# A decoder step on one core: the attention's results pass through DRAM, the modulation is spread over more products, one operand split is moved

## The chip, the cores and the metric

The program runs on one core of a Trainium2 chip. The metric is the device time of one execution in microseconds. A core has five engines with a queue of instructions each: PE (TensorE, matrix products), ACT (ScalarE), DVE (VectorE), POOL (GpSimd) and SP (SyncE, which here only issues transfers). ACT and POOL can issue transfers too. Results of PE land in PSUM, in banks; all other data on the chip lies in SBUF.

## The reference

One layer of a hybrid decoder, for 512 prompt tokens and 64 decoded tokens (8 sequences of 8), model width 1024:

- A modulation vector is made from the conditioning: `mod = silu(c) @ w_ada + b_ada`, cut into six parts of 1024 (shift, scale and gate of the first half of the layer, and of the second).
- `h = rmsnorm(x) * (1 + sc1) + sh1`, then one projection `h @ w_in`, cut into three operands of a gated convolution, queries, keys, values, and two gate logits.
- The convolution branch: `u = c_gate * xa`, a causal convolution of width 3 over tokens, times `b_gate`, then `@ w_conv_out` gives `ya`.
- The attention branch: 16 heads on 4 key heads, window 128, one learned sink for each head, distance bias; the result `o` (1024 wide) goes through `@ w_attn_out` to `yb`.
- `mixed = sigmoid(ga) * ya + sigmoid(gb) * yb`, and `x = x + g1 * (mixed @ w_mix_out)`.
- A second modulated norm, an up-projection to 2 x 2816, a convolution on one half, GELU, product with the other half, the down-projection, the gated residual, and a last norm.

All in float32. The decoded tokens also attend to a cache of 128 rows for each sequence.

## The kernel before

**Products.** PE has no full float32 product in one pass here. Each operand is split into a high part (rounded to PE's type) and a low part (what is left), and a product is three passes: high x high, high x low, low x high. `split` does it: one copy on ACT makes the high part, one subtraction on DVE the low part. Activations are kept transposed (features on the 128 partitions, the 576 tokens in the free dimension), so that 1024 features are 8 tiles of 128 x 576.

Most products are made in pairs by `pair_product` (a Winograd-like scheme: seven partial products of half size in place of eight). One pair makes two output tiles of 128 x 576 in seven parts, each of 4 x 3 matmuls of 288 columns into one of three banks X, Y and Z; after each part something is taken out of a bank (`minus`, `out_a0`, `out_b1` ...). The parts use sums and differences of weight halves (`pair_weights`, `prepare`) and of operand halves (`PairOperands`, `EarlyOperands`, `RawOperands`). The order is X a0, Z s1, Y s2, X a1, Y s3, Z s4, Y b1. A dictionary of steps says what ACT, DVE and POOL are given before the first part (key 0) and after each part (keys 1 to 7).

**The list of pairs.** `jobs` has 27 pairs (I number them from 0). Pairs 0 to 7 are gates and queries, 8 to 19 make the inner values and gates of the convolution, 20 to 22 the last gates, and 23 to 26 are `w_conv_out`. After them come eight plain products (`product`) with `w_attn_out`, which read the eight operands `o`, then the mix, the second norm and the feed-forward part. Pair n loads the weights of pair n + 2 and prepares those of pair n + 1.

**The filler.** Attention and modulation are written as generators. `pair_product` calls `tick(2)` once in each part, 14 ticks for a pair; `product` calls `tick` once for each of its 8 k. Each tick adds a rate to a counter, and for each whole number the generator runs one step. In the pairs the generator is `beside_conv`: the attention first (rates 0.28 and 0.45), then `modulation(2048)` at rate 0.6. The modulation reads 2048 columns of `w_ada` in 32 loads of 128 x 512 (256 KB), one for each step, and after every eight loads, five steps behind the last of them (`ROWS_AHEAD`), PE multiplies them (`side_by_side`, line 1264). The whole takes 44 steps. The second call, `modulation(4096)`, begins in pair 26, at rate 0.6.

**The buffers.** Nearly all temporary tiles come from one pool of 54 buffers of 128 x 576 float32 (`slot`, `A_BUFS`). A planner orders the instructions and hands out the buffers at build time: a buffer goes to the next tile in the order of the program, and the instruction that writes it first waits until all readers of the tile before are done. The queue of an engine is executed in order, so whatever stands behind such an instruction waits too. PE is held in the order of the program from the first pair on, ACT and DVE from pair 14 on (`N_ATT`). Weights have a pool of their own with 4 raw buffers (`W_BUFS`); an SP load of weights waits for one of them.

**The attention's results.** `prompt_values` (line 1160) writes the results of one key head for 4 blocks of 128 tokens into two tiles `ot`, eight in all, by ACT copies of 128 x 128 (line 1179). They are made in pairs 2 to 11. The decoded tokens' results go to a tile `od`. Both wait until pair 26, where `part_o` (line 1542) copies the 64 columns of `od` into each `ot` on POOL and splits it into `o` by ACT and DVE. So eight of the 54 buffers hold `ot` from the attention to pair 26.

**The early operands.** Before pair 0 a plain product makes the second query tile. Behind it stand four calls `op.n3()` (line 1495): each splits one quarter operand of `h` (128 x 288), which only the fifth part (Y s3) of the pairs reads.

Of the kernel before, what the change touches and what calls it, by code (L numbers as in the profile page):

```python
# [10 lines left out]
F32 = mybir.dt.float32  # L11
# [5 lines left out]
P = 128  # L17
D = 1024
NK = D // P
SEQ = 512  # L20
# [54 lines left out]
def step_kernel(ctx: ExitStack, tc: tile.TileContext, ins: dict, outs: list):  # L75
    nc = tc.nc
# [7 lines left out]
    dp = ctx.enter_context(tc.tile_pool(name="dp", bufs=1, space=bass.MemoryType.DRAM))  # L84
# [6 lines left out]
    def nm(s):  # L91
        cnt[0] += 1
        return f"{s}{cnt[0]}"

    def slot(s, dt=F32, shape=None):
        return ap_.tile(shape or [P, NT], dt, tag="a", name=nm(s))
# [7 lines left out]
    def aux():  # L104
        return pa.tile([P, 512], F32, tag="aux", name=nm("aux"))
# [25 lines left out]
    def pv(t):  # L131
        return t[:, 0:512]

    def sv(t):
        return t[:, 512:576]
# [7 lines left out]
    def split(hi, lo, src):  # L143

        act.activation(hi, src, AF.Copy)
        dve.tensor_tensor(out=lo, in0=src, in1=hi.bitcast(F32), op=ALU.subtract)

    def split_slot(src, s):
        hi, lo = slot(s + "h", F32R), slot(s + "l", F32R)
        split(hi, lo, src)  # L150
        return hi, lo
# [7 lines left out]
    def split_w(raw):  # L159
        nk = raw.shape[1]  # L160
        hi = wp.tile([P, nk, P], F32R, tag="whi", name=nm("whi"), bufs=S_BUFS)
        lo = wp.tile([P, nk, P], F32R, tag="wlo", name=nm("wlo"), bufs=S_BUFS)
        split(hi, lo, raw)
        return (lambda k: hi[:, k, :]), (lambda k: lo[:, k, :])
# [24 lines left out]
    filler = []  # L189
# [685 lines left out]
    def vt(i):  # L875
        return V[i // 2][:, i % 2, :]
# [6 lines left out]
    made, early_ops = {}, []  # L883
# [42 lines left out]
    def queries(t, q):  # L926

        hd, g2 = t // 2, t % 2
        for par in range(2):
            mine = HALF[par]  # L930
            dst = qS[:, hd // 2, :, :, par, g2, :] if par == hd % 2 else qX[:, hd // 2, :, :, g2, :]
            nc.vector.tensor_copy(
                out=dst[mine], in_=sv(q)[mine].rearrange("p (q b t) -> p q b t", q=2, b=4)
            )
        QS[t] = q
        ready[hd] = ticks[0] + Q_TICKS
        if g2 == 1:
            par = 1 - hd % 2
            for q in range(2):
                nc.gpsimd.dma_start(  # L940
                    qS[HALF[1 - par], hd // 2, q, :, par, :, :].rearrange("p b g t -> p b (g t)"),
                    qX[HALF[par], hd // 2, q].rearrange("p b g t -> p b (g t)"),
                )
# [20 lines left out]
        out=sel,  # L964
        in0=snk.rearrange("p (h g) -> p h g", h=4),
        in1=ind.unsqueeze(1).to_broadcast([P, 4, 4]),
        op=ALU.mult,
# [22 lines left out]


    pinned.append(pe)
    ot = []
    od = []

    def softmax_steps(s, n, sinks, nsinks, w):

# [161 lines left out]

    def prompt_values(parts):  # L1160
        O = aux()
        while len(ot) < 2 * parts[-1][0] + 2:
            ot.append(slot("ot"))
        for u, (hd, i, pts) in enumerate(parts):
            nkt, c = len(pts), slice(256 * u, 256 * u + 256)
            for n in range(2 * nkt):
                kt, par = n // 2, n % 2
                done = nc.tensor.matmul(  # L1168
                    O[HALF[par], c],
                    vt(i - nkt + 1 + kt)[:, hd * 64 : hd * 64 + 64],  # L1170
                    pts[kt][:, par * 256 : par * 256 + 256],
                    start=(kt == 0), stop=(kt == nkt - 1),
                )
                if u + n:
                    tc.keep_in_program_order(done)
        for u, (hd, i, pts) in enumerate(parts):
            for g in range(2):
                at = 256 * u + P * g
                nc.scalar.copy(ot[2 * hd + g][:, i * P : i * P + P], O[:, at : at + P])

    def attention():
        units = [(hd, i) for hd in range(4) for i in range(4)]
        s, pts = {}, {}
        for n in range(len(units) + 3):
            if n == CACHE_AT:
                cache_load(0)
            if n < len(units):
                hd, i = units[n]
                while 2 * hd + 1 not in QS or ticks[0] < ready[hd]:
                    yield False  # L1190
                s[n] = prompt_scores(hd, i)
            if n >= 4 and n % 2 == 0:
                prompt_values([(*units[u], pts.pop(u)) for u in (n - 4, n - 3)])
            yield False
            if 2 <= n <= len(units) + 1:
                pts[n - 2] = prompt_turn(units[n - 2][1], s.pop(n - 2))
            yield False
        filler[1] = .45
        before = None
        for n in range(3):  # L1200
            s, more = [], []
            if n < 2:
                yield from decode_scores(n, s, more)
            if before is not None:
                yield from before
            before = decode_values(n, s, more)
# [64 lines left out]
    def modulation(c0):  # L1271

        ps = aux()
        cols = [[None] * 4 for _ in range(NK)]
        for n in range(4 * NK + ROWS_AHEAD):
            if n < 4 * NK:
                k, j = n // 4, n % 4
                cols[k][j] = slot("ada", shape=[P, 512])
                c = c0 + 512 * j
                nc.sync.dma_start(cols[k][j], ins["w_ada"][0, k * P : k * P + P, c : c + 512])  # L1280
            yield False
            done = n + 1 - ROWS_AHEAD
            if done > 0 and done % 8 == 0:
                side_by_side(ps, (done // 4 - 2, done // 4 - 1), cols)
                yield False
        row = slot("row", shape=[P, 512])
        nc.scalar.copy(row, ps)
        yield False
        t = aux()
        yield False  # L1290
        for cc in range(4):
            transpose(t[:, cc * P : cc * P + P], row[:, cc * P : cc * P + P], ident)
        b0 = c0 // P
        nc.vector.tensor_tensor(
            out=modT[:, b0 : b0 + 16, :].rearrange("p (j c) r -> p j c r", j=4),
            in0=t.rearrange("p (c j r) -> p j c r", c=4, j=4)[:, :, :, 0:9],
            in1=parT[:, b0 : b0 + 16]
            .rearrange("p (j c) -> p j c", j=4)
            .unsqueeze(3)
            .to_broadcast([P, 4, 4, 9]),  # L1300
            op=ALU.add,
        )
        yield False
# [4 lines left out]

    def beside_conv():
        yield from attention()  # L1310
        filler[1] = .6
        yield from modulation(2048)
        yield True

# [79 lines left out]
    ya, w_next, raw_ao, o, late = [], {}, {}, [], []  # L1394
# [41 lines left out]
    def branch(m0, m1):  # L1436
        return Job(w_in, m0 * P, made, lambda: branch_outs(m0, m1), (m1 - m0) * P)

    def inner_job(m):
        return Job(w_in, 1024 + m * P, made, lambda: inner_outs(m), 1024)  # L1440

    def gate_job(n):
        x, c, m = (1, 5632, 2 * n) if n < 4 else (0, 4608, 2 * n - 8)
        return Job(w_in, c + m * P, made, lambda: gate_outs(x, m))

    def query_job(at):
        qt = [slot("q") for _ in range(2)]

        def outs():
            a0, a1, b0, b1 = copy_outs(qt, HD**-0.5)  # L1450

            def last(ps):
                b0(ps)
                for n in range(2):
                    queries(2 * at + n, qt[n])

            return a0, a1, last, b1

        return Job(w_in, Q0 + 2 * at * P, made, outs, scale=HD**-0.5)

    jobs = [
        gate_job(0), query_job(1), gate_job(1), gate_job(2), query_job(2), gate_job(3), gate_job(4),
        query_job(3), inner_job(0), inner_job(4), branch(0, 4), inner_job(1), inner_job(5), branch(1, 5),
        inner_job(2), inner_job(6), branch(2, 6), inner_job(3), inner_job(7), branch(3, 7),
        gate_job(5), gate_job(6), gate_job(7),
    ]
# [25 lines left out]
    q1 = slot("q")  # L1492
    nc.scalar.activation(q1, ps, AF.Copy, scale=HD**-0.5)
    queries(1, q1)
    for op in early_ops:
        op.n3()
    stT = state_in(st_conv, "stT", NK)
    a = aux()
    transpose(a[:, :74], par2, ident[:74, :74])
# [31 lines left out]
    for n in range(4):  # L1531
# [2 lines left out]
                1: [lambda n=n: late[2 * n - 2]()], 2: [lambda n=n: late[2 * n - 1]()],  # L1534
            }
    jobs[-1].after = {
        2: [lambda: part_o(2)], 3: [lambda: part_o(3)],
        4: [lambda: w_next.update({1: split_w(w_raw)})], 5: [lambda: part_o(4)], 6: [lambda: part_o(6)],
        7: [lambda: part_o(8)],
    }  # L1540

    def part_o(n):
        for k in range(len(o), n):
            nc.gpsimd.tensor_copy(out=sv(ot[k]), in_=od[0][:, k, :])
            o.append(split_slot(ot[k], "o"))

    for n, job in enumerate(jobs):
        if n == N_ATT:
# [490 lines left out]
    for m0, m1 in FCH:  # L2039
# [31 lines left out]
        if m1 < NF:  # L2071
# [3 lines left out]
            n = m1 - m0  # L2075
# [47 lines left out]
    jobs = [Job(w_dn[FB * P :, :], m * P, made3, lambda m=m: mix_outs(m, 40)) for m in range(0, NK - LATE, 2)]  # L2123
# [139 lines left out]
```

## Time and profile before

| | us |
|---|---|
| median of 3 runs (979.75 to 984.42) | 982.63 |
| the profiled execution | 978.47 |
| its span on the core | 976.7 |
| PE busy in the span | 944.2 |
| DVE busy | 723.6 |
| ACT busy | 571.7 |
| POOL busy | 143.3 |

The profile is one execution. The span is what the core's engines take; the profiled execution's own time is 1.8 us longer, the work around it. A row of the timeline gives the start, the duration, engine, line, operation, output and inputs, and in brackets how long the engine was idle ahead of it and what ended that. A row of the table of windows gives for each engine the busy time and the number of instructions, then the granted PE clock (1.00 is full), the share of the transfer engines' time and the rate. Matmul ends are modelled, so a stage is best read by the time from one matmul to the same one of the next pair.

### The profile page before, as it was taken

The numbers are of one execution on the slowest core, as the hardware profiler recorded it, in microseconds if no ns is written. First come the engines' busy times: TensorE is split into PE (matmuls) and PEld (weight loads), VectorE is DVE, ScalarE is ACT, GpSimd is POOL, SyncE is SP. The second block draws the span as 40 slices with busy tenths as digits, with TensorE's granted clock in tenths as the row PEclk, the third lists the DMA queues.
The fourth block names the chain that finished last, engine by engine and source line by source line (L and its number), as shares of the span: only waits on it lengthen the run. The fifth ranks groups of instructions, "written<-read, shape, count | busy, mean of one in ns | idle before, by whom it ended". The sixth has DMA issues, their size and how long they took to land.

```text
span 976.7 us, 18605 instructions
## 1 busy us (share of the span) xinstructions
PE 944.2 (97%) x7218; PEld 900.6 (92%) x7218; DVE 723.6 (74%) x1366; ACT 571.7 (59%) x1086; POOL 143.3 (15%) x320
## 2 busy tenths in 40 slices
PE   6999999999999987799999999999999999999997
PEld 4798989988999976799989999999999999999997
DVE  4787987879586664576677678995558998878874
ACT  5466687666666653587444658664225665547564
POOL 2221111022121311111001121100001000001110
PEclk9999999999999999899999999999999999999999
DMA  9976466543556898489986642233232333327542
GB/s 271 325 222 163 127 166 161 153 110 88 140 155 141 232 256 243 123 236 233 328 270 173 162 110 66 87 100 93 68 108 88 102 93 87 93 76 171 136 97 97
DMA packets 184138, 150.10 MB, mean 154 GB/s; under 512 B 7640, under 2 KB 162076, under 8 KB 183762
## 3 DMA queue, kind: packets, MB, share of 16 engines
q1 hardware_dynamic: 172546, 111.72, 38.5%
q0 software_dynamic: 11360, 36.94, 17.5%
q8 instruction: 56, 0.92, 0.4%
q14 instruction: 32, 0.26, 0.1%
q10 hardware_dynamic: 144, 0.26, 0.1%
HBM read 113.89 MB, written 12.07 MB: 129 GB/s over the span
## 4 chain that ended last, share of the span: by engine, by line
PE 88%; DMA 5%; ACT 4%; DVE 1%; issue 1%; SPq 0%; ACTq 0%; DVEq 0%; POOLq 0%
PE mm L117 50%; PE aux L117 35%; DMA ad<-in_w_ada 2%; PE aux L1264 1%; PE aux L1168 1%; ACT whi L117 1%; DMA ada<-in_w_ada 1%; ACT s L1009 1%; DMA raw<-in_w_in 1%; DMA x<-in_x_prompt 1%; ACT wlo L117 0%; DMA sg_dram<-sg 0%; DMA wl<-s 0%; DVE wlo L117 0%; ACT aux L117 0%
## 5 line engine op out<-in xcount | busy, mean ns | idle before, releaser
L117 ACT ACTIVATE whi<-raw 128x1024 fp32r<-128x1024 f32 (+3 forms) x192 | 194.8, 1023 | 113.4 <-DVE raw L117 35.3
L117 DVE TENSOR_TENSOR wlo<-raw,whi 128x1024 fp32r<-128x1024 f32 (+3 forms) x153 | 180.2, 1184 | 32.1 <-ACT whi L117 31.7
L117 DVE TENSOR_TENSOR raw<-raw 128x512 f32<-128x512 f32 x100 | 70.1, 701 | 2.5
L117 PE MATMUL aux<-2h,whi 128*128 128x288 f32 (+2 forms) x232 | 68.6, 296 | 0.0
L117 PE MATMUL aux<-2h,wlo 128*128 128x288 f32 (+2 forms) x232 | 68.5, 295 | 0.0
L117 PE MATMUL aux<-2l,whi 128*128 128x288 f32 (+2 forms) x232 | 68.5, 295 | 0.0
L117 POOL DMA_DIRECT2D wlo<-raw x39 | 34.4, 881 | 183.5 <-ACT wlo L117 64.7
L117 PE MATMUL aux<-hh,whi 128*128 128x288 f32 (+2 forms) x180 | 54.2, 308 | 0.0
L117 PE MATMUL aux<-hh,wlo 128*128 128x288 f32 (+2 forms) x180 | 52.7, 300 | 0.0
L117 PE MATMUL aux<-hl,whi 128*128 128x288 f32 (+2 forms) x180 | 52.7, 300 | 0.0
L117 PE MATMUL mm<-fh,wlo 128*128 128x256 f32 x224 | 47.7, 294 | 0.0
L117 PE MATMUL mm<-fh,whi 128*128 128x256 f32 x224 | 47.7, 294 | 0.0
L117 PE MATMUL mm<-fl,whi 128*128 128x256 f32 x224 | 47.1, 292 | 0.0
L117 PE MATMUL mm<-hh,whi 128*128 128x288 f32 (+2 forms) x160 | 45.4, 307 | 0.5 <-ACT hh L117 0.5
L117 PE MATMUL mm<-t,whi 128*128 128x288 f32 x184 | 40.0, 308 | 6.0 <-ACT mm L117 6.0
L117 PEld LDWEIGHTS aux<-2h,whi 128*128 128x128 f32 x232 | 43.6, 188 | 0.0
L117 PEld LDWEIGHTS aux<-2l,whi 128*128 128x128 f32 x232 | 43.6, 188 | 0.0
L117 PEld LDWEIGHTS aux<-2h,wlo 128*128 128x128 f32 x232 | 43.5, 188 | 0.0
L117 DVE SCALAR_TENSOR_TENSOR y<-pad,par2T,y 128x592 f32<-128x592 f32 x44 | 36.6, 833 | 9.0 <-ACT y L117 8.2
L117 PE MATMUL mm<-hh,wlo 128*128 128x288 f32 (+2 forms) x160 | 43.3, 295 | 0.0
L117 PE MATMUL mm<-hl,whi 128*128 128x288 f32 (+2 forms) x160 | 42.7, 298 | 0.0
L117 ACT ACTIVATE aux<-mm 128x288 f32<-128x288 f32 x50 | 19.9, 397 | 36.8 <-PE mm L117 36.0
(392 smaller groups left out, 3256.3 us busy)
## 6 DMA issues: line engine op xcount, KB each, us to landing
raw<-in_w_in SPq DMA_DIRECT2D x52, 512.0 KB, 4.0
raw<-in_w_up SPq DMA_DIRECT2D x44, 512.0 KB, 3.8
wlo<-raw POOLq DMA_DIRECT2D x33, 512.0 KB, 4.7
ada<-in_w_ada SPq DMA_DIRECT2D x64, 256.0 KB, 5.6
ad<-in_w_ada SPq DMA_DIRECT2D x32, 256.0 KB, 6.5
raw<-in_w_down SPq DMA_DIRECT2D x16, 512.0 KB, 4.0
sg_dram<-sg POOLq DMA_DIRECT2D x16, 288.0 KB, 3.8
gt<-sg_dram SPq DMA_DIRECT2D x16, 288.0 KB, 5.6
```

The source lines that it names most:

```text
L117: done = getattr(self.engine, name)(*args, **kwargs)
L1009: nc.scalar.activation(s[x // 2][:, x % 2, :w], s[x // 2][:, x % 2, :w], AF.Exp, bias=nmx[:, x : x + 1], accum_out=den[:, x : x + 1],)
L1168: done = nc.tensor.matmul(O[HALF[par], c], vt(i - nkt + 1 + kt)[:, hd * 64 : hd * 64 + 64], pts[kt][:, par * 256 : par * 256 + 256], start ...
L1264: done = nc.tensor.matmul(ps[32 * j : 32 * j + 32, :], cT[:, k, :], cols[k][j], start=(k == 1), stop=(k == NK - 2),)
```

## The change

Three things are changed.

1. When the fourth block of a key head is copied (`i == 3`), ACT issues a transfer of each of the two `ot` tiles to a DRAM tensor `ot_dram`. The tiles now have 512 columns (a buffer is taken all the same). In pair 26, `load_o` takes a buffer `o_raw`, loads the 512 columns back by SP and copies the decoded tokens' columns in by POOL; `part_o` splits from `o_raw` and then asks for the loads of the two tiles that come next. The first two loads stand at step 0 of pair 26.
2. `modulation(2048)` runs at rate 40/84 in place of 0.6: 6.67 steps for a pair in place of 8.4.
3. The four `n3` splits that stood ahead of pair 0 are now steps of pair 0: two behind its second part, two behind its third.

```diff
-    ot = []
-    od = []
+    ot, od = {}, []
+    ot_dram = dp.tile([NK, P, SEQ], F32, name="ot_dram")
...
-        while len(ot) < 2 * parts[-1][0] + 2:
-            ot.append(slot("ot"))
+        for k in range(2 * parts[-1][0], 2 * parts[-1][0] + 2):
+            if k not in ot:
+                ot[k] = slot("ot", shape=[P, SEQ])
...
                 nc.scalar.copy(ot[2 * hd + g][:, i * P : i * P + P], O[:, at : at + P])
+                if i == 3:
+                    nc.scalar.dma_start(ot_dram[2 * hd + g], ot[2 * hd + g])
...
-        filler[1] = .6
+        filler[1] = 40 / 84
         yield from modulation(2048)
...
-    for op in early_ops:
-        op.n3()
+    jobs[0].before = {2: [op.n3 for op in early_ops[:2]], 3: [op.n3 for op in early_ops[2:]]}
...
     jobs[-1].after = {
-        2: [lambda: part_o(2)], 3: [lambda: part_o(3)],
+        0: [lambda: load_o(2)], 2: [lambda: part_o(2)], 3: [lambda: part_o(3)],
         4: [lambda: w_next.update({1: split_w(w_raw)})], 5: [lambda: part_o(4)], 6: [lambda: part_o(6)],
         7: [lambda: part_o(8)],
     }
 
+    o_raw = []
+
+    def load_o(n):
+        for k in range(len(o_raw), n):
+            o_raw.append(slot("or"))
+            nc.sync.dma_start(pv(o_raw[k]), ot_dram[k])
+            nc.gpsimd.tensor_copy(out=sv(o_raw[k]), in_=od[0][:, k, :])
+
     def part_o(n):
         for k in range(len(o), n):
-            nc.gpsimd.tensor_copy(out=sv(ot[k]), in_=od[0][:, k, :])
-            o.append(split_slot(ot[k], "o"))
+            o.append(split_slot(o_raw[k], "o"))
+        load_o(min(n + 2, NK))
```

## The prediction

> **What bounds the kernel now.** I read the page first, then the waits of PE in order of time, then the stretch around the waits in windows of one pair, and there the queues of ACT, DVE and SP.
>
> ```profile
> PE 944.2 (97%) x7218; PEld 900.6 (92%) x7218; DVE 723.6 (74%) x1366; ACT 571.7 (59%) x1086; POOL 143.3 (15%) x320
> ...
> PE   6999999999999987799999999999999999999997
> ...
> PEclk9999999999999999899999999999999999999999
> ...
> PE 88%; DMA 5%; ACT 4%; DVE 1%; issue 1%; SPq 0%; ACTq 0%; DVEq 0%; POOLq 0%
> ```
>
> PE is busy nearly always and the chain that ended last is PE for 88%. The change takes no matmul away, so only the slices below 9 can pay: the first (the start, which the change does not touch), the three from 342 to 415 us, and waits too short to show here. The clock is down in the last of the three.
>
> ```profile
> 357.31 1.92 PE L1264 MATMUL aux<-ada,cT 128*32 128x512 f32 x16 [2.71 <-DMA ada<-in_w_ada]
> ...
> 372.43 1.92 PE L1264 MATMUL aux<-ada,cT 128*32 128x512 f32 x14 [1.59 <-DMA ada<-in_w_ada]
> ...
> 382.84 0.40 PE L117 MATMUL mm<-n4h,whi 128*128 128x288 f32 x1 [0.74 <-DVE sg L117]
> ...
> 391.32 0.54 PE L117 MATMUL mm<-t,whi 128*128 128x288 f32 x2 [3.42 <-ACT mm L117]
> ...
> 402.50 0.40 PE L117 MATMUL mm<-hh,wh 128*128 128x288 f32 x1 [4.39 <-ACT aux L117]
> ```
>
> Five waits, 12.85 us, all in pairs 19 to 21. The next table runs from the third part of one pair to that of the next (pairs 17 to 22, the last window to the end of pair 22's round).
>
> ```profile
> 330.00:343.14 13.14, 13.14 (x103) 11.54 (x101) 6.70 (x10) 8.58 (x13) 4.82 (x11) 1.00 0.93 265
> 343.14:359.16 16.02, 13.31 (x104) 11.64 (x100) 10.87 (x17) 7.41 (x12) 2.91 (x7) 1.00 0.93 246
> 359.16:374.27 15.11, 13.52 (x104) 11.80 (x100) 10.23 (x18) 7.93 (x13) 2.77 (x4) 1.00 0.97 273
> 374.27:391.32 17.05, 12.89 (x89) 11.41 (x87) 5.11 (x9) 5.72 (x10) 3.13 (x5) 1.00 0.78 214
> 391.32:412.55 21.23, 16.84 (x104) 15.04 (x105) 11.92 (x19) 9.29 (x15) 2.92 (x4) 0.84 0.52 133
> 412.55:424.00 11.45, 11.37 (x86) 11.13 (x85) 9.43 (x17) 10.41 (x21) 2.88 (x4) 1.00 0.71 167
> ```
>
> The first window is a pair with one batch of modulation and no wait: 13.14 us, of which the batch is 1.92, so a bare pair is 11.2. The next four take 69.4 us for four pairs and three batches (4 x 11.2 + 3 x 1.92 = 50.6; some 0.5 for the last transposes): 18.3 us are lost there. That is more than the 12.85 of waits, because the clock falls behind the longest (0.84 in the fifth window).
>
> What is late there is seen one queue further back:
>
> ```profile
> 389.04 0.68 ACT L117 ACTIVATE th<-tw 128x576 fp32r<-128x576 f32 x1 [7.12 <-DMA sg_dram<-sg]
> ...
> 397.34 0.76 DVE L117 TENSOR_TENSOR tl<-tw,th 128x576 fp32r<-128x576 f32 x1 [13.05 <-PE aux L1264]
> ...
> 384.41 8.75 SPq L1280 DMA_DIRECT2D ada<-in_w_ada  x2
> ...
> SPq L1280 <- DMA sg_dram<-sg: 7.0, 1, 7.0
> ...
> 352.53 0.38 SPq L156 DMA_DIRECT2D raw<-in_w_in  x1
> 353.00 1.48 SPq L1280 DMA_DIRECT2D ada<-in_w_ada  x3
> ```
>
> ACT's `th` reads `tw`, not `sg`, and yet waits 7.12 us for a transfer that reads `sg`; DVE's `tl` waits 13.05 us for modulation matmuls it has nothing to do with; a load of `ada` waits 7.0 us for `sg` too. These are waits for a buffer: the pool of 54 is empty. I counted in the program how many tiles of it are between first and last use: 61 at the worst in pair 20, 60 in 21, 58 in 22. At the 61: 16 of `h`, 4 `n4`, 8 `g`, 8 `ot`, 13 `ada`, 5 of the operands for `w_conv_out`, 7 others. The two waits for `ada` are another thing: SP stood at a weight load until 352.53, and the `ada` behind it came too late.
>
> **The change, part by part.** The base is the profiled execution, 978.47 us.
>
> *Buffers and rate (pairs 18 to 22).*
>
> ```profile
> L1179 ACT COPY ot<-aux x32: 243/272/302, 122.5 to 261.7; 128x128 f32<-128x128 f32 x32
> ...
> L117 ACT ACTIVATE oh<-ot x8: 668/674/676, 460.0 to 468.2; 128x576 fp32r<-128x576 f32 x8
> ```
>
> The eight `ot` are held from about 262 to 460 us and leave the pool in that time. Counting again with the loads of `ada` spread to 6.67 steps a pair (batches fall 1.37 pairs apart, at about 18.5, 19.9, 21.3 and 22.6 in place of 18.1, 19.2, 20.3, 21.3), the worst is 52 in pair 20, 57 just ahead of the third batch in 21, and 59 in 22, where eight `ada` now take the room of `ot`. So pair 20 fits, 21 lacks 3 in place of 6, 22 lacks 5 in place of 4. The last window shows that lacking 4 in pair 22 costs about 11.45 - 11.2 = 0.25 us. An `ada` is loaded five steps ahead: 5 / 8.4 of 11.2 = 6.7 us before, 5 / 6.67 of 11.2 = 8.4 us after, so 2.71 becomes about 1.0 and 1.59 nothing. Bounds: 18.3 us won when all fits, nothing when the shortage only moves on. I take 4.5 left (1.0 of `ada`, 3.5 for the shortages in 21 and 22, the size of one of the two long waits): **-13.8**.
>
> *The splits behind the first parts.*
>
> ```profile
> 68.00 0.45 ACT L117 ACTIVATE hh<-xn 128x288 fp32r<-128x288 f32 x1
> ...
> 70.94 0.43 ACT L117 ACTIVATE hh<-xn 128x288 fp32r<-128x288 f32 x1
> ...
> 72.87 0.45 DVE L117 TENSOR_TENSOR hl<-xn,hh 128x288 fp32r<-128x288 f32 x1
> ...
> 78.72 0.53 PE L117 MATMUL mm<-t,whi 128*128 128x288 f32 x1 [1.85 <-ACT mm L117]
> ...
> 78.00:80.00 2.00, 1.28 (x5) 1.28 (x6) 1.93 (x4) 1.51 (x5) 0.96 (x1) 0.71 0.85 246
> 80.00:82.00 2.00, 2.00 (x10) 2.00 (x10) 0.25 (x1) 0.01 (x1) 0.00 (x0) 0.50 1.08 213
> ```
>
> Four splits of 0.45 on ACT and 0.45 on DVE (1.8 us on each) leave the stretch ahead of pair 0, and pair 0's third part waits 1.85 us. The clock then drops: 1.28 x 0.29 + 2.00 x 0.50 = 1.4 us more. In their new place ACT and DVE are idle (0.01 and 0.25 of 2 us), and the fifth part needs them only one part later. Bounds: +1.8 (the fifth part waits for all four) and -3.2. ACT and DVE are ordered by the planner here, so I don't take all of it: **-2.0**. The Trainium skill ("TensorE: Matmul & The Clock Gate", section "HAM oscillation — how this bites in real kernels") ties the drop to idle gaps over about 3.4 us; the row shows half clock behind 1.85. By the page no clock is to be won here, and this term would be 0.9 smaller.
>
> *The transfers out.* Eight issues on ACT, each behind its copy.
>
> ```profile
> 150.00:200.00 50.00, 49.22 (x376) 45.47 (x375) 40.50 (x103) 37.53 (x98) 8.20 (x13) 1.00 0.52 140
> ...
> 971.60 0.40 ACTq L1805 DMA_DIRECT2D out<-yo  x1
> ```
>
> An issue of the same size takes ACT 0.40 us, 3.2 for all. ACT has 12.5 of 50 us free there and PE misses 0.8. Behind an issue stand the copies that empty PE's banks. Bounds 0 and +3.2; mostly covered: **+0.5**. The transfer engines are half free (0.52).
>
> *The transfers back (pair 26).*
>
> ```profile
> 454.28 0.37 SPq L156 DMA_DIRECT2D raw<-in_w_attn_out  x1
> ...
> 455.44 0.90 SPq L1280 DMA_DIRECT2D ada<-in_w_ada  x2
> 456.44 2.51 SPq L156 DMA_DIRECT2D raw<-in_w_attn_out  x2
> 459.52 4.34 SPq L1280 DMA_DIRECT2D ada<-in_w_ada  x5
> ...
> 461.50 0.67 ACT L117 ACTIVATE oh<-ot 128x576 fp32r<-128x576 f32 x1
> ...
> 464.86 0.45 DVE L117 TENSOR_TENSOR ya<-mm,p 128x288 f32<-128x288 f32 x1
> ...
> ada<-in_w_ada SPq DMA_DIRECT2D x64, 256.0 KB, 5.6
> ...
> 450.00:500.00 50.00, 50.00 (x381) 46.69 (x379) 35.08 (x47) 27.68 (x44) 1.36 (x2) 1.00 0.93 283
> ```
>
> PE misses nothing here before, so there is nothing to win. The first two loads can leave behind the weight load at 454.28 and land 5.6 us later, about 460.5: in time for the first split (460.0). The next two stand in SP's queue behind `ada` and the two weight loads that end at 458.95; they leave at about 459 and land at 464.6, where the third split ran at 461.50: 3.1 us late. Behind it, in order, stand on ACT a bank copy and a weight split, on DVE the sum at 464.86 that frees bank Y, and PE's last part waits for that bank. The later loads are covered by the last part and by the first product, which takes 1.74 us for each k and needs the eighth operand 12 us after its start. Bounds 0 and +7 (a second wave as late, and the clock); 2.1 MB more are also 7.4 us of transfers at 283 GB/s, in a stretch 0.93 full. I take **+3.0**. The Trainium skill ("DMA: Bandwidth & Descriptors", "Anatomy of one DMA — SWDGE (gpsimd) path") gives about 2.0 us and bytes / 436 GB/s, an estimate of 2.6 us for 256 KB; by that the loads come in time and the term is 0. The row says 5.6 in this traffic.
>
> The sum: 978.47 - 13.8 - 2.0 + 0.5 + 3.0 = 966.2. The median of the runs shown is 0.42% above the profiled execution, so I forecast 966.2 x 1.0042 = **970 us**.
>
> **The rivals**, on the median's scale.
>
> - *The shortage moves on.* The 59 tiles of pair 22 speak for it, the calm last window against. If 12 of the 18.3 us stay (about what the third and fourth of the four windows lose, 5.8 and 8.1, less the gain in pair 20): 978.
> - *It was the transfers, not the buffers* (the change does not do what it says): their share of 0.93 to 0.97 speaks for it, the 0.78 and 0.52 in the two worst windows against. Then only 3.3 us of the `ada` waits go: 978.47 - 3.3 - 2.0 + 0.5 + 3.0, or 981.
> - *Slower: the read-back is exposed.* Its loads are asked for in four waves in pair 26; if each wave's 5.6 us is waited out by ACT, DVE and then PE, that is 22.4 us, and 3.4 for the clock as in the fifth window (21.23 x 0.16): 25.8 in place of 3.0, or 993. It decides from three waves fully exposed (16.8 against the 15.3 won). SP runs ahead of ACT, which speaks against.
> - *Everything fits*: the bounds -18.3 and -3.2, nothing paid back but 0.5: 961.
>
> **How the numbers follow.** Forecast 0.52 (its own range 964 to 977), shortage moved 0.17, transfers 0.12, slower 0.11, all fits 0.08. About 0.5% is what can be told from no change here (977.7 to 987.5). Faster: 0.51 + 0.08 + half of 0.17 = 0.67; same: the rest of 0.17 and the 0.12, 0.21; slower 0.12. The range 962 to 985 leaves out the slower case and most of the lowest.
>
> **What would show it.** Right: the windows of pairs 18 to 22 at 11 to 13.5 us, no wait of ACT or DVE for `sg_dram` or line 1264, batches 15 us apart, no wait of PE at 78, one wait of about 3 us near 465 with ACT held by the load of `or`. Wrong: pairs 21 and 22 still over 15 us, or PE idle over 10 us between 455 and 480.

## The result, and the profile after

| | before | after |
|---|---|---|
| median, us | 980.32 (979.31 to 984.42, 11 runs) | 974.71 (973.25 to 977.77, 11 runs) |
| the profiled execution, us | 978.47 | 974.38 |
| its span, us | 976.7 | 972.6 |

The ratio is 0.9939, with an interval of 0.9924 to 0.9955: the change takes off 4.4 to 7.5 us. That is faster by 0.6%, a little more than the 0.5% that was named as the bound (the interval reaches down to 0.45%), and inside the range, but the gain is under half of the forecast one (970 of 982.63, or 1.3%). With the new runs the median of before is 980.32 in place of 982.63.

The page of the changed kernel: busy time by engine, PE and its clock in 40 slices, and the chain that ended last.

```profile
PE 944.0 (97%) x7218; PEld 900.2 (93%) x7218; DVE 723.5 (74%) x1366; ACT 572.3 (59%) x1086; POOL 142.5 (15%) x320
...
PE   7999999999999999897999999999999999999997
...
PEclk9999999999999999898999999999999999999999
...
PE 82%; DMA 7%; ACT 5%; DVE 2%; issue 2%; SPq 1%; POOL 0%; ACTq 0%; DVEq 0%; POOLq 0%
```

PE has the same work, and the dip around slices 17 to 19 is shallower but not gone. Transfers now carry 7% of the chain in place of 5%.

Three small waits return in both kernels at the same matmuls, so they can serve as marks. First their rows in PE's timeline before, then the longer waits of PE after (those of its start left out), with the same three marks among them (233.57, 427.38 and 534.90).

```profile
235.53 0.40 PE L117 MATMUL mm<-hh,wh 128*128 128x288 f32 x1 [0.77 <-ACT aux L117]
...
439.61 0.40 PE L117 MATMUL mm<-xh,wh 128*128 128x288 f32 x1 [0.90 <-ACT aux L117]
...
539.66 0.41 PE L117 MATMUL mm<-nh,wh 128*128 128x288 f32 x1 [0.22 <-ACT aux L117]
```

```profile
78.30 0.53 PE L117 MATMUL mm<-t,whi 128*128 128x288 f32 x2 [1.85 <-ACT mm L117]
...
233.57 0.40 PE L117 MATMUL mm<-hh,wh 128*128 128x288 f32 x1 [0.77 <-ACT aux L117]
...
357.29 1.93 PE L1267 MATMUL aux<-ada,cT 128*32 128x512 f32 x16 [1.46 <-DMA ada<-in_w_ada]
...
395.76 3.64 PE L1267 MATMUL aux<-ada,cT 128*32 128x512 f32 x16 [3.73 <-DMA ada<-in_w_ada]
...
427.38 0.41 PE L117 MATMUL mm<-xh,wh 128*128 128x288 f32 x1 [0.90 <-ACT aux L117]
...
458.53 0.61 PE L117 MATMUL mm<-nh,whi 128*128 128x288 f32 x1 [4.95 <-DVE ya L117]
...
534.90 0.41 PE L117 MATMUL mm<-nh,wh 128*128 128x288 f32 x1 [0.22 <-ACT aux L117]
```

The marks cut the span into four stages. I use them for every kernel below: the start with pairs 0 to 8, the pocket (where the first modulation's 32 loads lie), the read-back with the products behind it, and the rest.

| stage, us | before | after | difference |
|---|---|---|---|
| start to the first mark | 235.53 | 233.57 | -2.0 |
| pocket: first to second mark | 204.08 | 193.81 | -10.3 |
| read-back: second to third mark | 100.05 | 107.52 | +7.5 |
| third mark to the end | 437.0 | 437.7 | +0.7 |
| span | 976.7 | 972.6 | -4.1 |

So three quarters of what the pocket won went back at the read-back.

**The pocket.** The table of windows after, cut as it was for before, from the third part of pair 18 to that of pair 23.

```profile
341.20:352.50 11.30, 11.30 (x89) 11.30 (x86) 8.29 (x12) 5.37 (x10) 2.00 (x6) 1.00 0.86 233
352.50:367.40 14.90, 13.45 (x105) 11.74 (x103) 11.65 (x20) 7.95 (x12) 2.79 (x4) 1.00 0.96 275
367.40:380.60 13.20, 13.20 (x103) 11.60 (x101) 9.91 (x17) 10.17 (x18) 4.50 (x7) 1.00 0.98 253
380.60:399.30 18.70, 14.97 (x104) 11.79 (x100) 10.75 (x18) 8.28 (x13) 3.27 (x5) 0.87 0.92 269
399.30:411.90 12.60, 12.60 (x92) 12.57 (x89) 7.43 (x14) 9.63 (x19) 2.00 (x3) 0.93 0.68 172
```

Two of the five windows are near a bare pair (11.2) or a pair with a batch (13.14). The long waits of ACT and DVE for buffers (7.12 and 13.05 before) are gone; so is SP's 7.0 for `sg`. Three windows lose time. In 352.50 to 367.40 it is the 1.46 for `ada`. In 380.60 to 399.30 it is the 3.73 for `ada` and a clock of 0.87: the batch behind the wait takes 3.64 us in place of 1.92. In the last the clock is 0.93. The transfer engines are *busier* than before in the windows of pairs 20 and 21 (0.98 and 0.92, against 0.78 and 0.52), and yet the pairs are shorter.

Not every wait for a buffer is gone. One of 3.29 us is left on DVE, in pair 22: `xl` waits for a transfer of `s` into `wl`, neither of which it reads.

```profile
391.02 0.76 DVE L117 TENSOR_TENSOR xl<-g,xh 128x576 fp32r<-128x576 f32 x1 [3.29 <-DMA wl<-s]
```

PE does not wait for it: PE is busy until 392.03 and then stands at `ada`. That last wait has its reason in SP's queue. Rows of SP's timeline after, and two of the chain that ended last.

```profile
376.30 4.72 SPq L1283 DMA_DIRECT2D ada<-in_w_ada  x4
388.47 0.38 SPq L156 DMA_DIRECT2D raw<-in_w_conv_out  x1
388.94 1.09 SPq L1283 DMA_DIRECT2D ada<-in_w_ada  x2
...
380.08 8.25 DMA wlo<-raw
...
389.57 6.14 DMA ada<-in_w_ada
```

SP stands still from 381.02 to 388.47, held at a load of weights that waits for a raw buffer. The last two loads of the batch stand behind it, are issued by 390.03, and the batch can begin only at 395.76. The raw buffer is late in its turn because its reader, a transfer of `wlo<-raw` that POOL issues, takes 8.25 us, where the page has 4.8 in the middle. So busy transfer engines may still have a share in what is left; no run here separates it.

**The read-back.** SP, then ACT and DVE, in the stretch of pair 26; then the transfers of `or`, and three windows.

```profile
443.23 0.90 SPq L1549 DMA_DIRECT2D or<-ot_dram  x2
...
445.17 1.55 SPq L156 DMA_DIRECT2D raw<-in_w_attn_out  x2
446.81 4.21 SPq L1549 DMA_DIRECT2D or<-ot_dram  x2
...
454.93 0.68 ACT L117 ACTIVATE oh<-or 128x576 fp32r<-128x576 f32 x1 [4.84 <-DMA or<-ot_dram]
...
455.80 1.05 ACT L117 ACTIVATE whi<-raw 128x1024 fp32r<-128x1024 f32 x1
...
456.88 1.23 DVE L117 TENSOR_TENSOR wlo<-raw,whi 128x1024 fp32r<-128x1024 f32 x1 [0.48 <-ACT whi L117]
458.02 0.45 DVE L117 TENSOR_TENSOR ya<-mm,p 128x288 f32<-128x288 f32 x1
...
L1549 SPq DMA_DIRECT2D or<-ot_dram x8: 369/403/3739, 443.2 to 459.2; - x8
...
DMA to landing us min/median/max: 4.4/5.3/8.0
...
450.00:455.00 5.00, 3.51 (x25) 3.21 (x24) 0.58 (x1) 0.16 (x2) 0.47 (x2) 1.00 1.14 340
455.00:460.00 5.00, 1.47 (x6) 1.47 (x7) 3.88 (x6) 3.22 (x5) 0.00 (x0) 0.58 0.89 324
460.00:465.00 5.00, 5.00 (x31) 5.00 (x30) 1.47 (x3) 2.35 (x4) 0.00 (x0) 0.74 1.04 332
```

Read it from the top: the second two loads leave at 446.81, and the issue of the first of them takes 3.74 us by itself, so that it lands at 454.82, 8.0 us after its start. ACT waits 4.84 us for it. Only then come the weight split on ACT and the two subtractions on DVE, and behind these, at 458.02, the sum that frees bank Y. PE waits 4.95 us for it and then runs at a clock of 0.58 and 0.74. The transfer engines are full or nearly so all the while (1.14, 0.89, 1.04 of their time as the view counts it).

**The other two terms.** ACT's eight issues out, and the stretch around 78 us on ACT and PE after.

```profile
L1182 ACTq DMA_DIRECT2D ot_dram<-ot x8: 326/366/465, 138.4 to 260.3; - x8
...
70.53 0.43 ACT L117 ACTIVATE hh<-xn 128x288 fp32r<-128x288 f32 x1
...
73.78 2.96 ACT L117 ACTIVATE whi<-raw 128x1024 fp32r<-128x1024 f32 x3
76.78 1.06 ACT L117 ACTIVATE wlo<-whi 128x1024 fp32r<-128x1024 f32 x1
...
77.84 0.40 ACT L117 ACTIVATE mm<-mm 128x288 f32<-128x288 f32 x1
...
80.00:82.00 2.00, 2.00 (x17) 2.00 (x16) 0.00 (x0) 0.72 (x2) 0.00 (x0) 1.00 1.08 205
```

The issues take 0.37 us each, some 3 us of ACT in all, and PE's three small waits between 100 and 260 us are those of before to 0.01 us. At 78 the splits still stand ahead of pair 0 (the last `hh` at 70.53, 70.94 before) and PE waits the same 1.85 us. What differs is the clock behind it: 1.00 here, 0.50 before.

### The profile page after: what moved, and what is told of

It is laid out like the page before. It is cut to its first block, busy times and chain, and to the rows that moved or that the text cites. A ratio compares the mean times of both kernels' runs of the same rounds, so it can differ in the third digit from the quotient of the medians.

```text
span 972.6 us, 18634 instructions
## 1 busy us (share of the span) xinstructions
PE 944.0 (97%) x7218; PEld 900.2 (93%) x7218; DVE 723.5 (74%) x1366; ACT 572.3 (59%) x1086; POOL 142.5 (15%) x320
## 4 chain that ended last, share of the span: by engine, by line
PE 82%; DMA 7%; ACT 5%; DVE 2%; issue 2%; SPq 1%; POOL 0%; ACTq 0%; DVEq 0%; POOLq 0%
PE mm L117 46%; PE aux L117 34%; DMA ada<-in_w_ada 2%; PE aux L1267 2%; ACT whi L117 1%; DMA ad<-in_w_ada 1%; DMA wlo<-raw 1%; PE aux L1169 1%; DMA or<-ot_dram 1%; ACT s L1009 1%; DMA raw<-in_w_in 1%; DMA raw<-in_w_down 1%; ACT wlo L117 1%; SPq L531 1%; DMA out<-so 0%
## 5 line engine op out<-in xcount | busy, mean ns | idle before, releaser
L117 ACT ACTIVATE wlo<-whi 128x1024 fp32r<-128x1024 f32 (+1 forms) x39 | 40.0, 1025 | 0.8
```

The lines of the kernel that those rows point to most:

```text
L117: done = getattr(self.engine, name)(*args, **kwargs)
```

## The experiments

Every kernel's stages, by the same marks, in its profiled execution (us); the ratio is that of its timed runs to those of before on the same chip.

| kernel | first | pocket | read-back | median | ratio (95%) |
|---|---|---|---|---|---|
| before | 235.53 | 204.08 | 100.05 | 980.32 | |
| after | 233.57 | 193.81 | 107.52 | 974.71 | 0.9939 (0.9924 to 0.9955) |
| e1_dram_only | 233.26 | 192.73 | 107.60 | 974.20 | 0.9956 (0.9938 to 0.9975) |
| e2_early_back | 235.04 | 193.10 | 101.53 | 969.00 | 0.9890 (0.9862 to 0.9918) |
| e3_dram_only_early | 235.66 | 193.58 | 102.63 | 971.15 | 0.9908 (0.9879 to 0.9937) |
| e4_splits_only | 235.56 | 206.10 | 99.99 | 978.93 | 0.9998 (0.9979 to 1.0017) |
| e5_half | 233.14 | 191.37 | 107.41 | 971.96 | 0.9924 (0.9905 to 0.9942) |
| e6_ahead7 | 233.44 | 193.44 | 100.02 | 966.02 | 0.9857 (0.9821 to 0.9893) |
| e7_ada_on_act | 236.05 | 187.97 | 101.90 | 963.79 | 0.9829 (0.9792 to 0.9866) |
| e8_minus_first | 231.89 | 190.54 | 101.74 | 964.22 | 0.9834 (0.9798 to 0.9870) |
| e9_both | 230.83 | 187.96 | 102.41 | 962.08 | 0.9821 (0.9806 to 0.9836) |
| e10_both_ahead7 | 232.00 | 188.11 | 99.95 | 960.18 | 0.9802 (0.9785 to 0.9818) |

The theory after the result: the eight buffers are the whole gain; the read-back's 7.5 us are lost only because its loads are asked for too late; and what is left in the pocket is SP's order. The rivals: the slower rate shares in the gain; what is left is still a shortage (59 tiles wanted of 54); the lost time lies in the traffic itself.

### e1_dram_only: the way through DRAM alone

The change without its parts 2 and 3: the rate stays 0.6 and the four splits stand ahead of pair 0.

```diff
-        filler[1] = 40 / 84
+        filler[1] = .6
...
-    jobs[0].before = {2: [op.n3 for op in early_ops[:2]], 3: [op.n3 for op in early_ops[2:]]}
+    for op in early_ops:
+        op.n3()
```

> The change with the modulation left at 0.6 steps a tick and the four splits left where they were: only the way through DRAM. Theory (buffers): the most tiles wanted at once falls from 61 to 53 of 54, so the waits of ACT and DVE for sg_dram and for line 1264's matmuls are gone and the four windows of pairs 18 to 22 lose only what a late ada costs, 3 to 6 us in place of 18.3; with the read-back's 7.5 us the time is 970 to 976. Rival (transfers: the slower rate did the work): the pocket still loses over 12 us, and the time is 980 or more.

Measured: 974.20 us, within 0.5 us of the whole change. Its waits of PE for `ada` in the pocket and for bank Y:

```profile
354.81 1.93 PE L1267 MATMUL aux<-ada,cT 128*32 128x512 f32 x16 [2.48 <-DMA ada<-in_w_ada]
...
370.52 1.92 PE L1267 MATMUL aux<-ada,cT 128*32 128x512 f32 x14 [2.17 <-DMA ada<-in_w_ada]
385.73 1.92 PE L1267 MATMUL aux<-ada,cT 128*32 128x512 f32 x16 [0.73 <-DMA ada<-in_w_ada]
...
457.03 0.61 PE L117 MATMUL mm<-nh,whi 128*128 128x288 f32 x1 [4.69 <-DVE ya L117]
```

The pocket is 192.73, the read-back 107.60: both as in the change. At the old rate no wait of ACT or DVE for a transfer of `sg` or `s` or for the modulation's matmuls is left in the pocket. The rate only shifts the waits for `ada`: 5.38 us in three pieces here, 5.19 in two there.

### e4_splits_only: the moved splits alone

The kernel before with part 3 of the change and nothing else.

```diff
-    for op in early_ops:
-        op.n3()
+    jobs[0].before = {2: [op.n3 for op in early_ops[:2]], 3: [op.n3 for op in early_ops[2:]]}
```

> The kernel before with only the four splits moved behind the first parts. Theory (the planner issues them where it did, since their inputs are ready early, so each engine gets the same list): no difference, within 0.2%, and PE's wait of 1.85 us near 78 is there. Rival (the forecast's term): 2 to 3 us faster and no wait near 78.

Measured: ratio 0.9998 (0.9979 to 1.0017). The wait is where it was:

```profile
78.76 0.54 PE L117 MATMUL mm<-t,whi 128*128 128x288 f32 x2 [1.85 <-ACT mm L117]
```

In the two programs each engine's instructions stand in the same order, with the same operands: the planner issues the splits as soon as `xn` is there, wherever the program names them. Part 3 changes nothing. The 1.5 us that the change wins between that wait and the first mark (233.57 - 78.30 = 155.27, against 235.53 - 78.72 = 156.81 before) is the clock of one execution: here, without any other part of the change, it is 156.80.

### e2_early_back and e3_dram_only_early: ask for the results a pair earlier

e2 is the whole change with four loads in pair 25 and the rest at step 0 of pair 26; e3 is e1 with the same edit, so the two differ in rate and splits alone.

```diff
+    jobs[-2].after = {4: [lambda: load_o(4)]}
     jobs[-1].after = {
-        0: [lambda: load_o(2)], 2: [lambda: part_o(2)], 3: [lambda: part_o(3)],
+        0: [lambda: load_o(NK)], 2: [lambda: part_o(2)], 3: [lambda: part_o(3)],
```

> The whole change, but with four of the tiles read back from the fifth part of pair 25 on and the other four asked for at the start of pair 26. Theory (the reads come too late behind SP's queue and full transfer engines): PE's wait of 4.95 us near 458 and the slow clock behind it go, 4 to 7.5 us less than the change: 967 to 971. Rival (the reads cost because of their bytes, 2.1 MB in a stretch that is full already): the wait only moves, and the time stays within 2 us of the change, 973 to 977.

> The way through DRAM with the earlier reading, the modulation at 0.6 as before. If the slower rate is worth nothing once the buffers suffice, this is as fast as the early reading with the slower rate, 966 to 970; if the slower rate is what spares PE the waits for late ada loads, it is 3 to 5 us slower than that one.

Measured: 969.00 and 971.15 us. In e2 the read-back stage falls from 107.52 to 101.53, and the wait of 4.95 is gone. SP's rows, the landing of the eight loads, and a window of that stretch in e2:

```profile
433.07 2.74 SPq L1550 DMA_DIRECT2D or<-ot_dram  x4
...
445.54 1.80 SPq L1550 DMA_DIRECT2D or<-ot_dram  x4
...
DMA to landing us min/median/max: 4.8/5.5/6.1
...
450.00:455.00 5.00, 5.00 (x39) 4.88 (x38) 4.24 (x8) 3.77 (x7) 0.00 (x0) 1.00 1.09 356
```

The same loads take as long (5.5 in the middle) in the same full traffic (1.09 of the transfer engines' time, as the view counts it), and PE misses nothing: it is when they are asked for, not the traffic alone. The longest issue among them is 1.32 us here (1.43 in e3), against 3.74 in the change, so the earlier place gives more time and spares the long issue; these runs do not part the two. What stays of the 7.5 us is 1.5 in e2, a wait of 1.32 for the second modulation's `ada` in the first product. The pockets of e2 and e3 differ by 0.5 us, and the medians by 2.2 with overlapping intervals; e1 and the whole change differ by 0.5. So these runs show no gain of the slower rate clear of the noise. The rate alone, without the way through DRAM, was not tried.

### e5_half: is 57 of 54 still a shortage?

As e1, but only the tiles of key heads 0 and 1 go through DRAM; the four others keep their buffers, and the program then wants 57 of the 54 at the worst.

```diff
-                ot[k] = slot("ot", shape=[P, SEQ])
+                ot[k] = slot("ot", shape=[P, SEQ] if k < 4 else None)
...
-                if i == 3:
+                if i == 3 and hd < 2:
...
-            o_raw.append(slot("or"))
-            nc.sync.dma_start(pv(o_raw[k]), ot_dram[k])
+            o_raw.append(slot("or") if k < 4 else ot[k])
+            if k < 4:
+                nc.sync.dma_start(pv(o_raw[k]), ot_dram[k])
```

> As the run with only the way through DRAM (modulation at 0.6), but only four of the eight tiles go that way; the other four stay in their buffers. At the worst 57 tiles are wanted of 54. Theory (buffers): a part of the buffer waits comes back, so that the round from pair 18 to pair 23 lies between the 69.6 us of that run and the 81.0 us of the kernel before, near 74. Rival (a few tiles too many cost nothing, as in pair 22 before): it stays at 69 to 71 us. The second pair of loads is still late, so PE's wait near 457 stays at 4 to 5 us.

Measured: 971.96 us, ratio 0.9924. The pocket is 191.37, no worse than with all eight tiles out (192.73 in e1). Waits for buffers do come back, as the theory said; the longest:

```profile
387.21 0.46 DVE L117 TENSOR_TENSOR tw<-g 128x288 f32<-128x288 f32 x1 [4.13 <-DMA sg_dram<-sg]
```

ACT has one of 1.93 us for a transfer of `sg` too. But PE waits for neither, so three tiles wanted beyond the 54 cost no time that shows: a wait for a buffer on DVE is not yet time on PE. Four tiles fewer to read back do not help the other end: the stage is 107.41, with a wait of 4.72 at the same place, since the late second wave is still there.

### e6_ahead7: loads of the modulation two steps earlier

As e3, with a longer lead.

```diff
-ROWS_AHEAD = 5
+ROWS_AHEAD = 7
```

> Way through DRAM, early reading, rate 0.6, and each batch of the modulation multiplied seven steps behind its last load in place of five: 7/8.4 of 11.2 = 9.3 us of lead in place of 6.7. Theory (the loads of ada stand behind weight loads that wait for a raw buffer, some 9 us): PE's waits for ada of 2.41, 1.93, 0.42 and 2.58 us go, 4 to 7 us less than with five steps, 964 to 968. Rival (two tiles more, 55 of 54, bring buffer waits back): no gain or a loss, 970 or more.

Measured: 966.02 us, ratio 0.9857. The pocket did not move (193.44, 193.58 in e3); its waits for `ada` are 2.28, 1.94 and 0.33, where e3 has 2.41, 1.93 and 0.42. So a longer lead does not cure them. SP's loads of `ada` do wait 3.1 us for buffers of the modulation here (0.3 in e3), which may take a part of the lead away; but ahead of the first of these waits SP stands until 350.13 at a load of weights, whatever the lead. What the longer lead took away is the wait of the first product: 102.63 becomes 100.02, the level of before. The rest of the step from e3 is the first stage (235.66 to 233.44), whose clock differs from execution to execution.

### e7_ada_on_act: the modulation's loads past SP

As e2, but the first modulation's 32 loads are issued by ACT, so that no load of weights stands ahead of them.

```diff
-                nc.sync.dma_start(cols[k][j], ins["w_ada"][0, k * P : k * P + P, c : c + 512])
+                (nc.scalar if c0 == 2048 else nc.sync).dma_start(
+                    cols[k][j], ins["w_ada"][0, k * P : k * P + P, c : c + 512]
+                )
```

> Way through DRAM, early reading, rate 40/84, and the 32 loads of the first modulation issued by ACT in place of SP, so that they do not stand behind the weight loads. Theory (it is SP's order that makes ada late): PE's waits of 1.26 and 4.19 us and the slow clock behind the second go, 4 to 7 us less, 962 to 966. Rival (ada is late because the transfer engines are full, or the 32 issues of 0.4 us on ACT, 13 us, hold up the bank copies): within 2 us of 969, or slower.

Measured: 963.79 us, ratio 0.9829. The pocket falls from 193.10 to 187.97. Its waits of PE:

```profile
382.72 0.53 PE L117 MATMUL mm<-t,whi 128*128 128x288 f32 x2 [1.07 <-ACT mm L117]
394.93 1.92 PE L1267 MATMUL aux<-ada,cT 128*32 128x512 f32 x16 [0.75 <-DMA ada<-in_w_ada]
```

The 1.26 and 4.19 of e2 became one wait of 0.75, for a price of 1.07 where ACT is late with a copy: that copy stands behind two loads of `ada` which ACT can issue only at 381.27 and 381.69, when their buffers come free. So the place in SP's queue was the main cause: two steps more of lead did not help, another queue did.

### e8_minus_first: the wait at 78 us

As e2, but in pair 0 the weight split that stood ahead of the first copy of a bank is issued behind it (`minus` hands back its instruction for that).

```diff
-            after()
+            done = after()
             if at + 1 in steps:
-                steps[at + 1]()
+                with tc.issue_after(done.ins) if first_pair and at == 0 else ExitStack():
+                    steps[at + 1]()
```

> Way through DRAM, early reading, rate 40/84, and in pair 0 the weight split of step 1 held behind the first bank copy on ACT. Theory (that copy stands behind three weight splits and a moved copy, not behind the four operand splits): PE's wait of 1.85 us near 78 goes to below 0.5, 1.4 to 3.3 us less than 969. Rival (ACT is short of time there whatever the order): the wait stays or moves to the next part, 968 to 970.

Measured: 964.22 us, ratio 0.9834. ACT's rows:

```profile
74.05 2.02 ACT L117 ACTIVATE whi<-raw 128x1024 fp32r<-128x1024 f32 x2
...
76.06 0.42 ACT L117 ACTIVATE mm<-mm 128x288 f32<-128x288 f32 x1
76.39 1.06 ACT L117 ACTIVATE whi<-raw 128x1024 fp32r<-128x1024 f32 x1
```

The copy runs at 76.06 in place of 77.84, ahead of two weight pieces of 1.06 us, and PE's wait at 78 is gone. The first stage is 231.89, 1.3 us under the fastest with the wait (233.14) and 3.2 to 4.2 under those where the clock fell. So the wait came from the weights on ACT, not from the splits that the change meant to move. The median is 4.8 us under e2's, more than the 3.3 at the most that was expected. The rest lies in the pocket, where nothing was edited: 190.54 against 193.10, because the wait for `ada` of 4.19 is 2.71 in this execution and the clock behind it stays at 1.00. A part of e7's 5.1 us may be of that kind; the three kernels with the loads on ACT have pockets of 187.96 to 188.11, the seven that send `ot` through DRAM and load by SP 190.54 to 193.81.

### e9_both and e10_both_ahead7: put together

e9 is e7 with e8's edit; e10 has the lead of 7 as well.

> Way through DRAM, early reading, rate 40/84, the first modulation's loads issued by ACT, and pair 0's weight split held behind the first bank copy. If the two causes stand apart, the gains add: 969.0 less 5.2 (ACT's issues) less 4.8 (the copy) is 959; if both runs gained from the same thing, 962 to 964.

> As the run with both, and each batch seven steps behind its last load. Theory (what is left of the ada waits is lead): the waits of 0.75 us in pair 22 and 1.85 us in the first product go, 1 to 3 us less than the run with both. Rival (15 ada tiles in place of 13 bring buffer waits back, or the loads come no earlier since ACT issues in order): no difference or slower.

Measured: 962.08 (ratio 0.9821) and 960.18 us (0.9802, 0.9785 to 0.9818). The stages are those of the parts: no wait at 78, the pocket of e7, and in e10 the read-back at 99.95, where before has 100.05. But e9 missed the 959 that was expected of two causes that stand apart and came out at the edge of what was expected of one that both runs share: 2.6 of e8's gain lay in the pocket that e7 shortens too, and could not be had twice. In e10 the wait for `ada` in pair 22 stayed (0.69); the one in the first product went. The two intervals overlap, so the lead's 2 us is shown by the stage (102.41 to 99.95) and not by the medians. The page of e10:

```profile
PE   7999999999999999999999999999999999999997
...
PEclk9999999999999999999999999999999999999999
```

No slice between the ends is below 9 any more. e10 is 2.0% faster than before and, by the two ratios, 1.4% faster than the change.

## Why the prediction was half right

The forecast's sum was 966.2 on the scale of the profiled execution, which took 974.38. Taking the stages: -13.8 for the pocket against -10.3, +3.0 for the read-back against +7.5, -1.5 for the first stage (the splits and the issues) against -2.0, nothing for the rest against +0.7. That is 8.2 us, of which 8.0 lie in two terms.

- **Buffers, not transfers: right.** The three odd waits (7.12, 13.05 and 7.0) were waits for a buffer. They go with the eight tiles (e1), at the old rate, and (in the change) with the transfer engines busier than before. The rival that blamed the transfers for these three is refuted.
- **What is left in the pocket: wrong in kind.** I kept 4.5 us: 1.0 for `ada` and 3.5 for a shortage in pairs 21 and 22. A buffer wait near that size did come, 3.29 us on DVE in pair 22, but it cost PE nothing that shows (nor did e5's 4.13); and `ada` kept 5.19 us of waits (4.30 before) with 0.87 and 0.93 of clock behind them. The step that failed is "An `ada` is loaded five steps ahead: ... 5 / 6.67 of 11.2 = 8.4 us after". It counts the lead in the program, while SP's queue decides: I had quoted SP standing at a weight load until 352.53 and still let the lead cure it. e6 shows that two steps more of lead do not, e7 that another queue does, for 2.6 to 5.1 us (against e8's pocket and e2's). By the stages 18.3 - 10.3 = 8.0 us stayed, halfway between my 4.5 and the 12 of the rival "the shortage moves on", and by another cause than the rival's.
- **The slower rate: no term of its own.** I had no estimate that kept it apart from the buffers; e1 and e3 against the change and e2 show no gain of it clear of the noise.
- **The read-back: right in each step, too small.** It was to be a late second wave, then ACT, then DVE's sum, then PE at bank Y, and it was that. The time of issue is right as well: 459 of before less the 12.2 us by which the pair came sooner is 446.8, and the row says 446.81. The term that was mis-sized is the 5.6 us to land: the third load took 8.0, of which its issue alone was 3.74, so that ACT's split came 2.5 us later than forecast (454.93 against 452.4). Behind a wait of 4.95 the clock fell: 1.47 x 0.42 + 5.00 x 0.26 = 1.9 us in the two windows shown, most of the 2.5 that the stage lost beyond the wait. I had put the clock in the upper bound and not in the term; the measured 7.5 is 0.5 above that bound. The Trainium skill ("DMA: Bandwidth & Descriptors", section "Anatomy of one DMA — SWDGE (gpsimd) path") gave an estimate of 2.6 us. That section is on transfers issued by GpSimd and these are SP's; here 5.3 was the median and 8.0 the longest, for loads all of one size.
- **The slower rival's mechanism** needed three exposed waves; there was one.
- **The moved splits: wrong, -2.0 for nothing.** The step that failed is "Four splits ... leave the stretch ahead of pair 0". I wrote that the planner orders ACT and DVE here, and still took most of the gain. That the stage shows -2.0 all the same is luck: 0.4 of it lies ahead of the wait and 1.5 is the clock of that execution.
- **ACT's issues: 0 in place of 0.5.** They cost some 3 us of ACT and nothing on PE's path.

That 970 missed 974.71 by only 4.7 us owes 2 us to the scale: with the median of before over 11 runs the same sum gives 966.2 x 980.32 / 978.47 = 968.0.

## What to carry to other kernels

A tile that sits in a full pool from one phase to a far one can go through DRAM for almost nothing (here 3 us on an engine with room), if it is asked for back a pair earlier than the program needs it: here that was the difference between -6 and -11 us by the ratios of the change and of e2. A transfer that is late may be late by its place in the queue of the engine that issues it, as `ada` was here: look at what that queue is waiting for before lengthening a lead. And where a planner orders the instructions, a move in the program is a move on the chip only when the trace of an engine's order says so.

## What the hardware did that I had not expected

- **The same short wait costs clock in some executions and not in others.** In nine profiles PE waits 1.84 or 1.85 us near 78 us. In five (before, e2, e3, e4, e7) the clock then falls to between 0.50 and 0.58 for a stretch, in four (after, e1, e5, e6) it stays at 1.00. From that wait to the first mark the five take 156.79 to 156.81 us and the four 155.26 to 155.29: 1.53 us, all or nothing. In the clock records of the five traces one spell at half speed follows the wait, of 3.41 us each time. The waits for `ada` do the same: the clock fell behind 1.94 (e6), 2.31 (e4) and 2.41 us (e3), and not behind 2.48 (e1) and 2.71 (before, e8). Behind the longer waits for bank Y it fell in all three that I read (0.58 after 4.95 us, 0.54 after 4.69 in e1, 0.50 after 4.72 in e5), for 6.83 us each time. The Trainium skill ("TensorE: Matmul & The Clock Gate", section "HAM oscillation — how this bites in real kernels") names gaps over about 3.4 us; the long waits agree with it, while these runs show the loss at 1.85 us in five cases of nine. A single profile can't credit such a stretch to a change.
- **An issue took nearly as long as a transfer.** The issues of `or` on SP take 0.40 us in the middle and 3.74 at the longest, where the transfer engines were full (1.01 of their time and 318 GB/s from 447 to 451 us); the shortest of these transfers landed in 4.4. What stood behind it in SP's queue was issued from 450.66 on. The issue at the same place took 3.66 us in e1 and 3.50 in e5. Why it was held was not tried.
